# A transformer block with x transposed by the host, squares summed in place, part of w_in split by accumulating DMA, and three reordered blocks

## The chip, the cores and the metric

The kernel runs on one core of a Trainium2 chip, a few times, and each run gives the device's microseconds from start to end; the number compared is the median. One more execution is taken by the hardware profiler, and all profile lines below come from that one. Engines are named as in the profile: PE (matmul), PEld (its weight load), DVE (VectorE), ACT (ScalarE), POOL (GpSimd) and SP (SyncE, which issues most DMAs here).

## What is computed

One layer of a hybrid encoder on x of 256 x 2048, all in float32. `QK_COLS`, `ATT_WIDTH` and `CONV_CH` are 1024 columns each, so `w_in` is 2048 x 5120.

```python
xn = rms_norm(h, norm1_g[l])
proj = jnp.einsum('bsd,dn->bsn', xn, w_in[l])
q, k, v, ga, gg = jnp.split(proj, ...)
...
att = diff_attention(q, k, v, lam)          # q, k normed and rotated
u = causal_depthwise_conv(ga * sigmoid(gg), conv_w[l], conv_b[l])
u = silu(layer_norm(u, conv_ln_g[l], conv_ln_b[l]))
h = h + jnp.einsum('bsm,md->bsd', concat([att, u]), w_out[l])
hn = rms_norm(h, norm2_g[l])
a, bu = hn @ w_gate[l], hn @ w_up[l]        # 5632 hidden columns
h = h + (silu(a) * bu) @ w_down[l]
```

## The kernel before

**Precision.** [...] A product is hi x hi + lo x hi + hi x lo: three matmuls where one would do. The high part of a weight is a cast on ACT (`round_chunk`, L322), the low part a subtraction on DVE (`split_chunk`, L331). For chunks marked `by_dma` DVE is spared: ACT writes the negated high part into `wlo` (L325), and a DMA that adds, issued by POOL (L326), puts the raw weights on top.

**Chunks.** Weights are streamed in chunks of 512 KB: two blocks of 128 rows by 512 columns. Chunk 0 to 31 are the conv columns of `w_in` (four blocks of eight chunks, gate and value columns side by side, hence two loads each), 32 to 79 k, q and v, 80 to 111 `w_out`, 112 to 127 the first gate and up block. A chunk is 12 matmuls of 512 columns: eight with the high part (L361, L362), then four with the low part (L367). `run_chunks` records, for each step t, the loads, casts and subtractions of chunks ahead (two ahead, one in the first eight) and then the multiplication of chunk t; each engine runs its own list in that order. `resume` is called twice in a chunk and lets generators go on; that is how transposes, the attention and the convolution's steps are slipped between chunks.

**Buffers.** A raw chunk lies in one of five `raw` buffers; from chunk 8 on every third one lies in pool `early` (tag `wb`, two buffers) instead. There are three `whi` and three `wlo`. A load waits on SP until the last reader of its buffer is done, and all loads behind it wait too.

**The opening.** x is loaded in its rows, in five parts; PE transposes it block by block (`x_part`, L441, 32 transposes), and ACT and DVE split it, scaled by the norm's gain (`split_scaled`, L235, L236). The gains are a row table that PE transposes (L157), as are the conv weights (L184). 14 and then 5 transposes of nothing keep PE busy before the first data (L145). ACT sums squares from the rows (L430).

**The convolution** is 30 taps for each of eight channel tiles on DVE (L512, tile `y`). They are dealt out by a credit: 1.30 us a half chunk, of which a subtraction on DVE takes its part (`spend`).

**The feed-forward part** uses fast products: a *pair* chunk (kind s, `multiply_pair`) loads rows of two weight matrices (tile `wb`), forms four sums of them on DVE (`wt`, L963 to L965), casts them on ACT (`wh`) and subtracts on DVE (`wlb` L972, `wlt` L973): seven products of three matmuls (L990 to L992). Plain chunks of the two matrices are kinds g and u (`multiply_two`, L1011, L1012, L1017). `ORDER`, `FIRST_ORDER` (block 1) and `DORDERS` (down passes behind each group of gate/up blocks) say in which order the kinds come. After blocks 0 to 3, 4 to 7 and 8 to 10 stands a down pass; its results are added to the residual in DRAM by accumulating DMAs from POOL (L1135, L1152). `BY_DMA` names the g and u chunks that are split by DMA.

Of the kernel before, what the change touches and what calls it, by code (L numbers as in the profile page):

```python
# [12 lines left out]
F32 = mybir.dt.float32  # L13
# [5 lines left out]
P = 128  # L19
# [30 lines left out]

WARM = (14, 5)

XPARTS = (range(0, 2), range(2, 4), range(4, 8), range(8, 12), range(12, 16))

OPENING = KD // NK
# [24 lines left out]
ORDER = "sggsggsuusuu"  # L80
FIRST_ORDER = "gsgsggsuusuu"


HD = N // P
ND = 2
DORDERS = {4: ("gguuggsguugsuu", "sgggugggusuuuu"), 3: ("gguusggsuu", "ggsggsuuuu")}

# [23 lines left out]
def tile_block(  # L111
    ctx: ExitStack,
    tc: tile.TileContext,
    x, w_in, conv_w, w_out, w_gate, w_up, w_down, gains, vecs, rope, out,
):
# [30 lines left out]

    warm_up(WARM[0])

    rows = pre.tile([NR, P], F32, tag="rows", name="rows", bufs=1)
    act.dma_start(out=rows, in_=gains)  # L150

    act.copy(small.tile([P, 8], F32, tag="rsq", name="first"), neghalf)
    cols = const.tile([P, NR], F32, tag="cols", name="cols")

    def gain_columns():
        ps = aux_ps.tile([P, N], F32, tag="aux", name="ps_cols")
        pe.transpose(ps[:, :NR], rows, ident[:NR, :NR])  # L157
        act.copy(cols, ps[:, :NR])
# [6 lines left out]
    neg_lam = const.tile([P, 1], F32, tag="neg_lam", name="neg_lam")  # L165
    cw_rows = [pre.tile([W, N], F32, tag="va", name="cw_rows") for _ in range(CC // N)]
    rt = pre.tile([P, NM, 2, DH], F32, tag="vb", name="rt")
# [3 lines left out]
    def late_loads():  # L171
        flat = conv_w.rearrange("o w i c -> (o w i) c")
        for i in range(CC // N):
            sp.dma_start(out=cw_rows[i], in_=flat[:, i * N : (i + 1) * N])
        for t, v in ((gb, vecs[:2]), (lamv, vecs[2:])):
            sp.dma_start(out=t, in_=v.rearrange("(o v) d -> o v d", o=1).to_broadcast(list(t.shape)))
        sp.dma_start(out=rt, in_=rope.rearrange("(m p) c d -> p m c d", p=P))

    def late_constants():
        late_loads()  # L180
        yield from lag(4)
        pw = aux_ps.tile([P, N], F32, tag="aux", name="ps_cw")
        for ct in range(NCT):
            pe.transpose(pw[:, ct * W : (ct + 1) * W], cw_rows[ct * P // N][:, ct * P % N : ct * P % N + P], ident[:W, :W])  # L184
        act.copy(cw.rearrange("p c w -> p (c w)"), pw[:, : NCT * W])
        while not normed:
# [132 lines left out]

    def round_chunk(c):  # L320
        c["hi"] = c["view"](wp.tile([P, NK * N], F32R, tag="whi", name="whi", bufs=HL_BUFS))
        act.copy(c["hi"], c["raw"])  # L322
        if c["by_dma"]:
            c["lo"] = c["view"](wp.tile([P, NK * N], F32R, tag="wlo", name="wlo", bufs=HL_BUFS))
            act.activation(c["lo"], c["raw"], AF.Copy, scale=-1.0)  # L325
            pool.dma_start(out=c["lo"], in_=c["raw"].bitcast(F32R), accum_op=ALU.add)  # L326

    def split_chunk(c):
# [60 lines left out]
    def run_chunks():  # L389
# [35 lines left out]
    rstd1 = [const.tile([P, 1], F32, tag=f"rstd1_{m}", name=f"rstd1_{m}") for m in range(NM)]  # L425
    ss1 = [small.tile([P, D // N], F32, tag=f"ss1_{m}", name=f"ss1_{m}", bufs=1) for m in range(NM)]

    def square_sum(src, accum, **kw):
        junk = pre.tile([P, N], F32, tag="junk", name="junk", bufs=1)
        act.activation(junk[:, : src.shape[-1]], src, AF.Square, accum_out=accum, **kw)  # L430

    def x_load(ks):
        cs = slice(ks[0] * P, (ks[-1] + 1) * P)
        for m in range(NM):
            sp.dma_start(out=h[m][:, cs], in_=x[m * P : (m + 1) * P, cs])

    def x_part(ks):
        for k in ks:
            ps = aux_ps.tile([P, N], F32, tag="aux", name="ps_x")
            for m in range(NM):  # L440
                pe.transpose(ps[:, m * P : (m + 1) * P], h[m][:, k * P : (k + 1) * P], ident)  # L441
            xT[k] = lhs_pair("x", k)
            split_scaled(xT[k], ps[:, :S], col("g1", k))

    def x_rest():
        c = 0
        for part in XPARTS[1:]:
            while chunks_done[0] < (part[0] // NK) * 2 - 1:
                yield
            x_part(part)  # L450
            yield
            yield
            if part[-1] % (N // P) == N // P - 1:
# [608 lines left out]
    def gate_up_block(j):  # L1062
# [170 lines left out]
```

## Time and profile before

| | |
|---|---|
| median of 3 runs | 1063.49 us (1062.6 to 1063.9) |
| profiled execution, its own time | 1060.47 us |
| its span, first to last instruction | 1058.7 us |
| granted TensorE clock over the span | 0.998 |
| HBM read, written | 202.14 MB, 9.44 MB |

A timeline row is: start in us, duration, engine, line, operation, tile written <- tiles read, shapes, count; in brackets the engine's idle time just before and what ended it. A row of waits is: us in total, how often, the longest. A row of windows gives for each engine the busy time and the number of instructions, then the granted clock, the mean busy share of the DMA engines and GB/s. Durations of matmuls overlap, so the pace of PE is read from starts. Packets of DMA under 2 KB were 25806 of 123470.

### The profile page before, as it was taken

How to read it: one execution, taken by the hardware profiler on the slowest of the kernel's cores; microseconds unless marked ns; L12 is line 12 of the kernel's file. 1: busy time of each engine (PE TensorE's matmuls, PEld its weight loads, DVE VectorE, ACT ScalarE, POOL GpSimd, SP SyncE). 2: the span in 40 equal slices, each digit the busy share in tenths (PEclk: the TensorE clock that was granted, in tenths of full speed). 3: DMA queues.
4: the chain of work that ended last, by engine and by line, in shares of the span. 5: the costliest groups of instructions: out<-in, count | busy, mean ns of one | idle time of the engine just before them, and what ended most of it. 6: DMA issues, size and time to landing. Idle time of an engine off the chain costs nothing.

```text
span 1058.7 us, 13117 instructions
## 1 busy us (share of the span) xinstructions
PE 1042.8 (99%) x4702; PEld 857.3 (81%) x4702; DVE 892.2 (84%) x1087; ACT 626.3 (59%) x802; POOL 104.5 (10%) x147
## 2 busy tenths in 40 slices
PE   9999999999999999999999989999999999999998
PEld 7888888877888777888888878888888878888876
DVE  5799989899666699899687888989878788889896
ACT  6644567755766565676453656666654456667442
POOL 0030122211100100000001100000000110010010
PEclk9999999999999999999999999999999999999999
DMA  9755555553546566987857698879856889798692
GB/s 300 232 179 194 199 171 171 176 170 133 176 171 226 183 228 205 292 254 223 250 186 226 202 293 246 266 207 277 259 172 226 237 209 295 211 296 251 173 280 95
DMA packets 123470, 231.33 MB, mean 219 GB/s; under 512 B 7956, under 2 KB 25806, under 8 KB 123404
## 3 DMA queue, kind: packets, MB, share of 16 engines
q1 hardware_dynamic: 113904, 201.61, 56.3%
q0 software_dynamic: 9440, 28.84, 14.0%
q8 instruction: 37, 0.61, 0.2%
q14 instruction: 29, 0.24, 0.1%
q10 hardware_dynamic: 60, 0.03, 0.0%
HBM read 202.14 MB, written 9.44 MB: 200 GB/s over the span
## 4 chain that ended last, share of the span: by engine, by line
PE 83%; DVE 7%; DMA 3%; issue 3%; ACT 2%; POOL 2%; DVEq 0%; POOLq 0%; ACTq 0%
PE q L1017 11%; PE q L1011 11%; PE q L1012 11%; PE acc L367 9%; PE acc L362 9%; PE acc L361 9%; PE q L992 7%; PE q L990 7%; PE q L991 7%; DVE wlo L331 2%; DMA wlo<-raw 2%; DVE y L512 1%; PE ps_a L828 1%; ACT whi L322 1%; PE ps_o L724 1%
## 5 line engine op out<-in xcount | busy, mean ns | idle before, releaser
L322 ACT CAST whi<-raw 128x1024 fp32r<-128x1024 f32 x272 | 282.6, 1051 | 162.9 <-PE acc L362 56.7
L331 DVE TENSOR_TENSOR wlo<-raw,whi 128x1024 fp32r<-128x1024 f32 x234 | 283.7, 1225 | 87.5 <-ACT whi L322 85.6
L969 ACT CAST wh<-wt 128x2048 fp32r<-128x2048 f32 x52 | 99.6, 1915 | 63.4 <-DVE wt L965 62.9
L973 DVE TENSOR_TENSOR wlt<-wt,wh 128x2048 fp32r<-128x2048 f32 x52 | 119.1, 2290 | 15.0 <-ACT wh L969 14.7
L361 PE MATMUL acc<-whi,xhi 128*128 128x512 f32 x320 | 126.3, 395 | 0.5 <-ACT whi L322 0.5
L1011 PE MATMUL q<-whi,chi 128*128 128x512 f32 x320 | 125.7, 393 | 0.0
L362 PE MATMUL acc<-whi,xlo 128*128 128x512 f32 x320 | 125.0, 391 | 0.2 <-DVE xlo L236 0.2
L1012 PE MATMUL q<-whi,clo 128*128 128x512 f32 x320 | 124.8, 390 | 0.0
L990 PE MATMUL q<-wh,fhi 128*128 128x512 f32 x280 | 109.9, 393 | 0.0
L991 PE MATMUL q<-wh,flo 128*128 128x512 f32 x280 | 109.0, 389 | 0.0
L512 DVE SCALAR_TENSOR_TENSOR y<-upad,cw,y 128x256 f32<-128x256 f32 x240 | 102.8, 490 | 0.0
L1011 PE MATMUL q<-whi,ahi 128*128 128x512 f32 x256 | 100.2, 391 | 0.0
L1012 PE MATMUL q<-whi,alo 128*128 128x512 f32 x256 | 99.7, 389 | 0.0
L972 DVE TENSOR_TENSOR wlb<-wb,wh 128x1536 fp32r<-128x1536 f32 x52 | 91.1, 1753 | 5.3 <-ACT wh L966 5.3
L1017 PE MATMUL q<-wlo,chi 128*128 128x512 f32 x320 | 86.8, 393 | 5.7 <-DMA wlo<-raw 5.7
L367 PE MATMUL acc<-wlo,xhi 128*128 128x512 f32 x320 | 87.7, 396 | 0.9 <-DVE wlo L331 0.8
L966 ACT CAST wh<-wb 128x1536 fp32r<-128x1536 f32 x52 | 76.7, 1474 | 0.0
L1017 PEld LDWEIGHTS q<-wlo,chi 128*128 128x128 f32 x320 | 60.3, 189 | 19.3 <-DMA wlo<-raw 6.9
L326 POOL DMA_DIRECT2D wlo<-raw x38 | 32.8, 864 | 402.0 <-ACT wlo L325 209.5
L361 PEld LDWEIGHTS acc<-whi,xhi 128*128 128x128 f32 x320 | 60.1, 188 | 13.5 <-ACT whi L322 0.8
L362 PEld LDWEIGHTS acc<-whi,xlo 128*128 128x128 f32 x320 | 60.1, 188 | 13.2 <-DVE xlo L236 1.0
L1011 PEld LDWEIGHTS q<-whi,chi 128*128 128x128 f32 x320 | 60.4, 189 | 12.5
(229 smaller groups left out, 1782.4 us busy)
## 6 DMA issues: line engine op xcount, KB each, us to landing
raw<-in_w_down_dram SPq DMA_DIRECT2D x64, 512.0 KB, 7.4
raw<-in_w_in_dram SPq DMA_DIRECT2D x48, 512.0 KB, 4.6
raw<-in_w_gate_dram SPq DMA_DIRECT2D x48, 512.0 KB, 7.2
raw<-in_w_up_dram SPq DMA_DIRECT2D x48, 512.0 KB, 6.4
wb<-in_w_up_dram SPq DMA_DIRECT2D x40, 512.0 KB, 3.8
wb<-in_w_gate_dram SPq DMA_DIRECT2D x40, 512.0 KB, 5.0
wlo<-raw POOLq DMA_DIRECT2D x38, 512.0 KB, 6.8
raw<-in_w_in_dram SPq DMA_DIRECT2D x64, 256.0 KB, 5.6
```

Of the source, the lines that this page charges most:

```text
L322: act.copy(c["hi"], c["raw"])
L331: dve.tensor_tensor(c["lo"], c["raw"], c["hi"].bitcast(F32), ALU.subtract)
L361: pe.matmul(ps[m], xhi[:, ms], hi[:, j, :], start=c["first"] and j == 0, stop=False)
L362: pe.matmul(ps[m], xlo[:, ms], hi[:, j, :], start=False, stop=False)
L367: pe.matmul(ps[m], xhi[:, ms], lo[:, j, :], start=False, stop=c["last"] and j == nk - 1)
L512: dve.scalar_tensor_tensor(y[:, ct, :], src, wk, y[:, ct, :], ALU.mult, ALU.add)
L973: dve.tensor_tensor(lot, c["t"], c["hi"][:, :SUMMED].bitcast(F32), ALU.subtract)
L990: pe.matmul(ps, hi, c["hi"][:, w], start=bool(first), stop=False)
L991: pe.matmul(ps, lo, c["hi"][:, w], start=False, stop=False)
L1011: pe.matmul(ps, xs[i][0][:, ms], hi[:, i, :], start=i == 0 and bool(c["first"].get(qs[m])), stop=False)
L1012: pe.matmul(ps, xs[i][1][:, ms], hi[:, i, :], start=False, stop=False)
L1017: pe.matmul(sum_bank(c, qs[m]), xs[i][0][:, ms], lo[:, i, :], start=False, stop=i == 1 and bool(c["last"].get(qs[m])))
```

## The change

The host hands in x a second time, transposed and laid out by partition (`xt`), and the gains and conv weights as columns, so that no transpose of these is left. x's own rows, which the residual needs, are loaded ahead of chunks 20, 22, 24 and 26. Chunk 0 is loaded in halves, one of each from SP and ACT, and its first half is cast on DVE. The squares are taken in place of the transposed x once it is split, added up by DVE over blocks, and four matmuls with a column of ones give the sums, after chunk 10. Ten w_in chunks (16, 22 to 70) are *far*: loaded seven chunks ahead, cast and negated by ACT five chunks ahead into a `wb` buffer (tile `far`), with the low part by an accumulating DMA from POOL. No chunk before 76 uses `wb` for raw weights any more. The order of kinds in block 1 and in the second half of the last down pass has one g more ahead of a pair, and blocks 4 and 8, right behind a down pass, have no g chunk split by DMA.

```diff
-WARM = (14, 5)
+WARM = 18
+SUMS_AT = 20
+XROWS = (20, 22, 24, 26)
...
-FIRST_ORDER = "gsgsggsuusuu"
+FIRST_ORDER = "gsggsgsuusuu"
...
-DORDERS = {4: ("gguuggsguugsuu", "sgggugggusuuuu"), 3: ("gguusggsuu", "ggsggsuuuu")}
+DORDERS = {4: ("gguuggsguugsuu", "sgggugggusuuuu"), 3: ("gguusggsuu", "gggsgsuuuu")}
...
+FAR = (16, 76, 6)
+FAR_AHEAD = (7, 5)
...
-    warm_up(WARM[0])
-    rows = pre.tile([NR, P], F32, tag="rows", name="rows", bufs=1)
-    act.dma_start(out=rows, in_=gains)
...
+    warm_up(WARM)
     cols = const.tile([P, NR], F32, tag="cols", name="cols")
+    act.dma_start(out=cols, in_=gains)
...
     def late_loads():
-        flat = conv_w.rearrange("o w i c -> (o w i) c")
-        for i in range(CC // N):
-            sp.dma_start(out=cw_rows[i], in_=flat[:, i * N : (i + 1) * N])
+        sp.dma_start(out=cw, in_=conv_w)
...
-        pw = aux_ps.tile([P, N], F32, tag="aux", name="ps_cw")
-        for ct in range(NCT):
-            pe.transpose(pw[:, ct * W : (ct + 1) * W], cw_rows[ct * P // N][:, ct * P % N : ct * P % N + P], ident[:W, :W])
-        act.copy(cw.rearrange("p c w -> p (c w)"), pw[:, : NCT * W])
...
     def load_chunk(c):
...
+        if c is chunks[0]:
+            for k in range(NK):
+                x_load(range(k, k + 1))
+                for q, (col, n) in zip((sp, act), c["cols"]):
+                    q.dma_start(out=c["raw"][:, k, o : o + n], in_=rows[:, k, col : col + n])
+                    o = (o + n) % c["width"]
+            return
...
     def round_chunk(c):
...
+        if c is chunks[0]:
+            act.activation(small.tile([P, 8], F32, tag="rsq", name="first"), neghalf, AF.Sigmoid)
+            dve.tensor_copy(c["hi"][:, 0], c["raw"][:, 0])
+            x_part(range(NK))
+            act.copy(c["hi"][:, 1], c["raw"][:, 1])
+            return
+        if c in chunks[:OPENING]:
+            x_part(range(c["k0"], c["k0"] + NK))
...
+    def round_far(c):
+        t = early.tile([P, 2, NK * N], F32R, tag="wb", name="far")
+        c["hi"], c["lo"] = c["view"](t[:, 0]), c["view"](t[:, 1])
+        act.copy(c["hi"], c["raw"])
+        act.activation(c["lo"], c["raw"], AF.Copy, scale=-1.0)
+        pool.dma_start(out=c["lo"], in_=c["raw"].bitcast(F32R), accum_op=ALU.add)
...
+            for ahead, do in ((FAR_AHEAD[0], load_chunk), (FAR_AHEAD[1], round_far)):
+                if t + ahead < n and chunks[t + ahead].get("far"):
+                    do(chunks[t + ahead])
...
+    xraw = [early.tile([P, HK, S], F32, tag="wb", name="xraw") for _ in range(KD // HK)]
     def x_load(ks):
-        cs = slice(ks[0] * P, (ks[-1] + 1) * P)
-        for m in range(NM):
+        k = ks[0]
+        sp.dma_start(out=xraw[k // HK][:, k % HK : k % HK + len(ks), :], in_=xt[:, k : k + len(ks), :])
+    def x_rows(i):
+        XW = D // len(XROWS)
+        for m in range(NM):
+            cs = slice(i * XW, (i + 1) * XW)
             sp.dma_start(out=h[m][:, cs], in_=x[m * P : (m + 1) * P, cs])
     def x_part(ks):
         for k in ks:
-            ps = aux_ps.tile([P, N], F32, tag="aux", name="ps_x")
-            for m in range(NM):
-                pe.transpose(ps[:, m * P : (m + 1) * P], h[m][:, k * P : (k + 1) * P], ident)
             xT[k] = lhs_pair("x", k)
-            split_scaled(xT[k], ps[:, :S], col("g1", k))
+            split_scaled(xT[k], xraw[k // HK][:, k % HK, :], col("g1", k))
     def x_rest():
...
+        for k in range(0, KD, 4):
+            while chunks_done[0] < k + 2:
                 yield
+            act.activation(four(k), four(k), AF.Square)
+            yield
+            if k >= HK:
+                add(four(0), four(k - 4 if k == HK else k))
+                yield
+        add(four(0), four(HK))
...
+        add(t[:, :2], t[:, 2:4])
+        while chunks_done[0] < SUMS_AT:
+            yield
+        ps = aux_ps.tile([P, N], F32, tag="aux", name="ps_ss")
+        for m in range(NM):
+            for k in range(2):
+                pe.matmul(ps[:, m * 8 : m * 8 + 8], t[:, k, m * P : (m + 1) * P], ones, start=k == 0, stop=k == 1)
...
-                   BY_DMA if j > 1 else dict(g=(), u=BY_DMA["u"]))
+                   BY_DMA if j > 1 and j not in FIRSTS else dict(g=(), u=BY_DMA["u"]))
...
+    for i in range(*FAR):
+        chunks[i].update(far=True, load=lambda c: None, round=lambda c: None, split=lambda c: None)
+    last_far = FAR[1] - OPENING
     for i, c in enumerate(chunks[OPENING:-12]):
-        c["spare_raw"] = i % 3 == 2
+        c["spare_raw"] = i % 3 == 2 and i >= last_far
...
+    for i, t in enumerate(XROWS):
+        before[t] = lambda i=i: x_rows(i)
...
+    given["xt"] = given["xt"].T.reshape(KD, P, S).transpose(1, 0, 2)
+    given["conv_w"] = given["conv_w"].reshape(W, NCT, P).transpose(2, 1, 0)
```

PE's list in the opening, before, from within chunk 0 to the first matmul of chunk 1 (`xhi`, `xlo`: the parts of x; `h`: x's rows; `ps_x`: their transposes):

```order
L361 MATMUL acc<-whi,xhi_149 128x512
L362 MATMUL acc<-whi,xlo_150 128x512
L441 MATMUL ps_x<-ident,h_81 128x128
L441 MATMUL ps_x<-ident,h_82 128x128
L441 MATMUL ps_x<-ident,h_81 128x128
L441 MATMUL ps_x<-ident,h_82 128x128
L367 MATMUL acc<-wlo,xhi_149 128x512 x4
L361 MATMUL acc<-whi,xhi_193 128x512
```

And the same place in the change:

```order
L378 MATMUL acc<-whi,xhi_153 128x512
L379 MATMUL acc<-whi,xlo_154 128x512
L384 MATMUL acc<-wlo,xhi_153 128x512 x4
L378 MATMUL acc<-whi,xhi_167 128x512
L379 MATMUL acc<-whi,xlo_168 128x512
```

The four transposes between the high and the low half of chunk 0 are gone; eight more go from each of three later chunks.

DVE's list at the start of block 4, right behind the first down pass, before: the end of the first pair's low parts, the last sums of the down pass (L1151), and the second pair:

```order
L973 TENSOR_TENSOR wlt<-wt,wh 128x2048
L1151 TENSOR_TENSOR sum_5407<-q_5209,sum_5407 128x512
L1151 TENSOR_TENSOR sum_5409<-q_5274,sum_5409 128x512
L963 TENSOR_TENSOR wt<-wb 128x1024
L964 TENSOR_TENSOR wt<-wb,wt 128x512
L965 TENSOR_TENSOR wt<-wt,wb 128x512
L972 TENSOR_TENSOR wlb<-wb,wh 128x1536
L973 TENSOR_TENSOR wlt<-wt,wh 128x2048
```

And in the change:

```order
L1011 TENSOR_TENSOR wlt<-wt,wh 128x2048
L348 TENSOR_TENSOR wlo<-raw,whi 128x1024
L1189 TENSOR_TENSOR sum_5344<-q_5146,sum_5344 128x512
L1189 TENSOR_TENSOR sum_5346<-q_5211,sum_5346 128x512
L348 TENSOR_TENSOR wlo<-raw,whi 128x1024
L1001 TENSOR_TENSOR wt<-wb 128x1024
L1002 TENSOR_TENSOR wt<-wb,wt 128x512
L1003 TENSOR_TENSOR wt<-wt,wb 128x512
L1010 TENSOR_TENSOR wlb<-wb,wh 128x1536
L1011 TENSOR_TENSOR wlt<-wt,wh 128x2048
```

The two g chunks' subtractions stand ahead of the second pair's low parts.

SP's loads around chunk 28, a far one, in the change, with the semaphores that each waits for (DMASW2 is that of chunk 28's accumulating DMA; DVE, of a subtraction; two rows a chunk while the chunk is two loads of 256 columns; the row of 512 columns is the far chunk 34, and behind it come chunks 29, 30 and 31):

```order
L317 DMA raw<-in_w_in_dram 128x2x256 [waits DMAHW5_49,DVE_49]
L317 DMA raw<-in_w_in_dram 128x2x256 [waits DMAHW6_49]
L317 DMA raw<-in_w_in_dram 128x2x512 [waits DMAHW7_49,DVE_49]
L317 DMA raw<-in_w_in_dram 128x2x256 [waits DMAHW0_49,DMASW2_49,Activation_49]
L317 DMA raw<-in_w_in_dram 128x2x256 [waits DMAHW1_49]
L317 DMA raw<-in_w_in_dram 128x2x256 [waits DMAHW2_49,DVE_49]
L317 DMA raw<-in_w_in_dram 128x2x256 [waits DMAHW3_49]
```

Before, loads waited for DVE's subtractions alone; now the load of chunk 29 waits for the landing of chunk 28's low part. The same holds for chunks 47 and 59 behind 46 and 58; behind the far chunks 16, 22, 34, 52 and 64 it is the load of the chunk after the next.

More of the change, by code (lines that the diff above doesn't have):

```diff
@@ L113, in tile_block @@
     tc: tile.TileContext,
-    x, w_in, conv_w, w_out, w_gate, w_up, w_down, gains, vecs, rope, out,
+    x, xt, w_in, conv_w, w_out, w_gate, w_up, w_down, gains, vecs, rope, out,
 ):
@@ L145, in warm_up @@
             pe.transpose(warm[:, :P], ident, ident)
-    warm_up(WARM[0])
-    rows = pre.tile([NR, P], F32, tag="rows", name="rows", bufs=1)
-    act.dma_start(out=rows, in_=gains)
-    act.copy(small.tile([P, 8], F32, tag="rsq", name="first"), neghalf)
+    warm_up(WARM)
     cols = const.tile([P, NR], F32, tag="cols", name="cols")
[L155 to L158, printed above, removed]
+    act.dma_start(out=cols, in_=gains)
     def col(key, k):
@@ L165, in tile_block @@
     neg_lam = const.tile([P, 1], F32, tag="neg_lam", name="neg_lam")
-    cw_rows = [pre.tile([W, N], F32, tag="va", name="cw_rows") for _ in range(CC // N)]
     rt = pre.tile([P, NM, 2, DH], F32, tag="vb", name="rt")
@@ L425, in tile_block @@
     rstd1 = [const.tile([P, 1], F32, tag=f"rstd1_{m}", name=f"rstd1_{m}") for m in range(NM)]
-    ss1 = [small.tile([P, D // N], F32, tag=f"ss1_{m}", name=f"ss1_{m}", bufs=1) for m in range(NM)]
     def square_sum(src, accum, **kw):
@@ L1204, in tile_block @@
         before[part[0] // NK] = lambda part=part: x_load(part)
-    before[0] = lambda: (x_load(XPARTS[0]), gain_columns(), x_part(XPARTS[0]), warm_up(WARM[1]), start(x_rest()))
+    before[0] = lambda: start(x_rest())
+    for i, t in enumerate(XROWS):
+        before[t] = lambda i=i: x_rows(i)
     before[OPENING] = lambda: start(late_constants())
     run_chunks()
-_FLAT = {"x": (S, D), "w_in": (D, 5120), "conv_w": (1, W, 1, CC), "w_out": (D, D), "w_gate": (D, FF),
+_FLAT = {"x": (S, D), "xt": (S, D), "w_in": (D, 5120), "conv_w": (1, W, 1, CC), "w_out": (D, D), "w_gate": (D, FF),
          "w_up": (D, FF), "w_down": (FF, D)}
@@ L1219 @@
     arrays, args = {}, []
-    given = {name: np.asarray(inputs[name]).reshape(shape) for name, shape in _FLAT.items()}
-    given["gains"] = np.concatenate([np.asarray(inputs[name]).reshape(n, P) for name, _, n in ROWS])
+    given = {name: np.asarray(inputs["x" if name == "xt" else name]).reshape(shape) for name, shape in _FLAT.items()}
+    given["xt"] = given["xt"].T.reshape(KD, P, S).transpose(1, 0, 2)
+    given["conv_w"] = given["conv_w"].reshape(W, NCT, P).transpose(2, 1, 0)
+    given["gains"] = np.concatenate([np.asarray(inputs[name]).reshape(n, P) for name, _, n in ROWS]).T
     given["vecs"] = np.concatenate([np.asarray(inputs[name]).reshape(1, DH) for name in VECS])
```

18 lines of the change are left out of this document (8 added, 10 removed).

## The prediction, made before the changed kernel was run

> **What bounds the kernel now.** I read the page first, then who TensorE waits for.
>
> ```profile
> span 1058.7 us, 13117 instructions
> PE 1042.8 (99%) x4702; PEld 857.3 (81%) x4702; DVE 892.2 (84%) x1087; ACT 626.3 (59%) x802; POOL 104.5 (10%) x147
> PE q L1017 <- DMA wlo<-raw: 5.7, 3, 3.0
> PE q L992 <- DVE wlt L973: 1.9, 2, 1.0
> PE acc L367 <- DVE wlo L331: 0.8, 1, 0.8
> ```
>
> PE is busy 99% of the span, so a microsecond counts only if it leaves PE's queue: a matmul or transpose less, or a wait less. The three waits shown are 8.4 us. Next, the timeline gives PE's pace: from a pair's first matmul to the next chunk stand 21 matmuls (7 products of 3).
>
> ```profile
> 875.71 0.39 PE L990 MATMUL q<-wh,fhi 128*128 128x512 f32 x1
> 880.47 0.39 PE L1011 MATMUL q<-whi,chi 128*128 128x512 f32 x1
> ```
>
> 4.76 us / 21 = 0.227 us each: a chunk of 12 takes 2.72 us, a pair 4.76. The change has the same number of such matmuls, so I look for places where PE kept another pace.
>
> **1. The opening.** Timeline and one window, from the warm-up to the first matmul of chunk 8:
>
> ```profile
> 0.72 0.54 ACTq L150 DMA_DIRECT2D rows<-in_gains_dram  x1
> 0.72 3.33 DMA rows<-in_gains_dram
> 1.35 3.25 PE L145 MATMUL ps_warm<-ident 128*128 128x128 f32 x14 [1.35 <-POOL neghalf L139]
> 7.43 0.50 PE L361 MATMUL acc<-whi,xhi 128*128 128x512 f32 x1 [0.51 <-ACT whi L322]
> 12.24 1.05 ACT L322 CAST whi<-raw 128x1024 fp32r<-128x1024 f32 x1 [1.60 <-DMA raw<-in_w_in_dram]
> 13.09 1.03 PE L441 MATMUL ps_x<-ident,h 128*128 128x128 f32 x8
> 13.88 1.18 PE L367 MATMUL acc<-wlo,xhi 128*128 128x512 f32 x4
> 15.08 0.49 PE L361 MATMUL acc<-whi,xhi 128*128 128x512 f32 x1
> 33.65 0.39 PE L361 MATMUL acc<-whi,xhi 128*128 128x512 f32 x1
> 7.43:33.65 26.22, 25.96 (x124) 20.85 (x125) 17.03 (x25) 19.40 (x39) 2.35 (x4) 1.00 0.94 299
> ```
>
> Chunks 0 to 7 take 26.2 us where 8 x 2.72 = 21.8 would do; 28 of the 32 transposes stand in there, eight in 13.88 - 13.09 = 0.79 us, so 2.8 us. They go. The warm-up becomes 18, which by 14 in 3.25 us ends near 5.5 us, so chunk 0 can begin about 2 us earlier; the gains (landed at 4.05 us) and ACT's two further DMA issues of half a microsecond stand beside the warm-up. But the row at 12.24 says that chunk 2's weights come by DMA, and the bytes ahead of them stay the same (x is only transposed); the window's DMA share is 0.94. So I let DMA set chunk 2: cast at 12.24 to 13.3, matmuls at 13.3 instead of 15.08. From there six chunks need 16.3 us: chunk 8 at 29.6, **4.0 us earlier**. Bounds: without any DMA wait chunk 8 comes at 5.5 + 21.8 = 27.3 (6.3 us); 2.4 us if a wait there is followed by a spell of slow clock, whose 1.6 us is worked out in part 4. The squares (four of 1024 columns instead of eight of 512) and DVE's four adds (three of 1024 columns, one of 512; a subtraction of 1024 takes 1.2 us in part 2, so 4.3 us) hide beside this: ACT is busy 19.4 and DVE 17.0 of 26.2 us. Without that cover the adds would cost those 4.3 us, but they are spread over five chunks. The x rows that the residual needs come later, by SP, and nobody reads them before the output projection.
>
> ```profile
> 38.28 0.68 PE L184 MATMUL ps_cw<-ident,cw_rows 31*128 31x31 f32 x8
> 38.89 1.20 PE L367 MATMUL acc<-wlo,xhi 128*128 128x512 f32 x4
> ```
>
> The eight conv-weight transposes, 0.6 us, go; four ps_ss matmuls come, which no row shows: 0.08 us each by these (0.3 in all), 0.1 by the transposes above. Net **0.2 us**, between 0 and 0.6.
>
> **2. Every sixth w_in chunk by DMA.** DVE loses ten subtractions of 1.2 us. They were hidden, since PE waited for a wlo only once, at 217.8, where DVE's taps stood ahead of it.
>
> ```profile
> 216.62 1.27 DVE L512 SCALAR_TENSOR_TENSOR y<-upad,cw,y 128x256 f32<-128x256 f32 x3
> 217.80 1.22 DVE L331 TENSOR_TENSOR wlo<-raw,whi 128x1024 fp32r<-128x1024 f32 x1
> 219.08 1.19 PE L367 MATMUL acc<-wlo,xhi 128*128 128x512 f32 x4 [0.84 <-DVE wlo L331]
> ```
>
> PE's step there was 1.0 us too long. Chunk 70 now leaves DVE, and taps end earlier since a far chunk spends no credit: **1.0 us**, bounds 0 and 1.2. What it adds: two ACT passes, a POOL issue and a DMA, each far ahead.
>
> ```profile
> L326 POOL DMA_DIRECT2D wlo<-raw x38: 845/862/936, 416.1 to 978.6; - x38
> DMA to landing us min/median/max: 4.7/6.8/11.7
> 51.08 1.06 ACT L322 CAST whi<-raw 128x1024 fp32r<-128x1024 f32 x1 [1.67 <-PE acc L362]
> 57.23 0.39 PE L361 MATMUL acc<-whi,xhi 128*128 128x512 f32 x1
> raw<-in_w_in_dram SPq DMA_DIRECT2D x64, 256.0 KB, 5.6
> ```
>
> A chunk's cast (16 in these rows) starts 6.15 us ahead of its matmuls; a far one stands three chunks earlier in ACT's order, 14.3 us ahead. After two ACT passes of 1.06 us and the median landing of 6.8 its low part is there 5.4 us early. But its raw buffer is held till then, and in three places (chunks 29, 47, 59) the load of the very next chunk waits for it on SP, with all later loads behind: 5.6 us plus a cast of 1.06 end 1.3 us after the far chunk's start, 1.5 us before they are needed. In five more the load is that of the chunk after, with 4.2 us to spare. So nothing, if landings stay under 8.3 us.
>
> **3. Two orders.** In both blocks a pair's first wlt was late.
>
> ```profile
> 403.86 2.29 DVE L973 TENSOR_TENSOR wlt<-wt,wh 128x2048 fp32r<-128x2048 f32 x1 [0.31 <-ACT wh L969]
> 406.21 0.50 PE L992 MATMUL q<-wlt,fhi 128*128 128x512 f32 x1 [1.03 <-DVE wlt L973]
> 1026.79 2.29 DVE L973 TENSOR_TENSOR wlt<-wt,wh 128x2048 fp32r<-128x2048 f32 x1
> 1029.13 0.50 PE L992 MATMUL q<-wlt,dhi 128*128 128x512 f32 x1 [0.88 <-DVE wlt L973]
> ```
>
> One g chunk more ahead of the pair gives PE 2.72 us and costs DVE one wlo, 1.2. The waits of 1.0 and 0.9 (steps 1.2 and 1.0 too long) go. The next pair then follows after one g only: DVE needs 1.2 + 0.7 + 0.7 + 1.75 + 2.3 + 0.3 (ACT) + 1.2 = 8.15 us per pair and g, PE 33 x 0.227 = 7.5; of the 0.65 the lead just won covers most. **1.6 us**, bounds 0.9 (nothing covered, twice) and 2.2.
>
> **4. No accumulating DMA for g in the blocks behind a down pass.** The two long waits are there.
>
> ```profile
> 612.29 0.39 PE L1012 MATMUL q<-whi,clo 128*128 128x512 f32 x1
> 615.71 1.20 PE L1017 MATMUL q<-wlo,chi 128*128 128x512 f32 x4 [3.03 <-DMA wlo<-raw]
> 867.63 0.39 PE L1012 MATMUL q<-whi,clo 128*128 128x512 f32 x1
> 870.46 2.07 PE L1017 MATMUL q<-wlo,chi 128*128 128x512 f32 x4 [2.44 <-DMA wlo<-raw]
> 873.89 0.40 PE L1011 MATMUL q<-whi,chi 128*128 128x512 f32 x1
> 605.89 0.39 PE L990 MATMUL q<-wh,fhi 128*128 128x512 f32 x1
> 606.02 1.28 DVE L1151 TENSOR_TENSOR sum<-q,sum 128x512 f32<-128x512 f32 x2
> 611.87 2.29 DVE L973 TENSOR_TENSOR wlt<-wt,wh 128x2048 fp32r<-128x2048 f32 x1 [0.31 <-ACT wh L969]
> ```
>
> The first costs 3.2 us and a second short wait behind it 0.3. The second costs 2.6, and then eight matmuls take 873.89 - 870.46 = 3.43 us instead of 1.82: 1.6 us at half pace. Together 7.7 us. What is late next: DVE gets two wlo ahead of the second pair, so its wlt ends at 614.2 + 2.4 = 616.6, and PE asks for it at 605.89 + (21 + 24 + 2) x 0.227 = 616.6. I give back 0.2 each: **7.3 us**, bounds 5.2 (a whole wlo of 1.25 us late in each block) and 7.7.
>
> [...] These rows differ: 2.44 us sufficed once, 3.03 us did not. [...]
>
> **Sum.** 4.0 + 0.2 + 1.0 + 1.6 + 7.3 = 14.1 us, from the profiled execution's 1060.5 to 1046.4. The median shown is 1063.5, 3.0 above it; I keep that distance: **1049.4 us**.
>
> **Rivals.**
> - *The opening meets the slow clock.* PE now waits for chunks 1 and 2, about a microsecond each; if that halves the pace once, as at 870, the opening gains 2.4 instead of 4.0: 1051.0. For it: the wait at 12.24. Against: at 615 nothing followed. Chance 0.17.
> - *The raw buffers become the wait.* 2 MB of x rows are loaded over chunks 20 to 26 as well. If landings take 10 us there, the three next-chunk loads are 1.7 us late, and with a slow clock after each 3.3: 1059.3. Chance 0.10.
> - *Slower than before.* The same place: at 11.1 us per landing three waits of 2.8 + 1.6 us eat 13.2 us and the five two-behind places begin; at the longest landing seen, 11.7, it is 3 x 5.0 + 5 x 0.7 = 18.5 us: 1067.9. It decides at about 11.2 us; the median of 6.8 speaks against. Chance 0.05.
> - *Nothing moves net*: DVE is the next bound behind the down passes and in both orders, so that sections 3 and 4 bring half (4.5 us) and the far chunks lose the rest: 1063. Chance 0.04.
>
> **How the numbers follow.** Forecast 0.64, rivals as given. 0.2% (2.1 us) is about what can be told from no change: faster 0.91, same 0.04, slower 0.05. The range: all upper bounds (6.3 + 0.6 + 1.2 + 2.2 + 7.7 = 18.0) give 1045.5, a slow clock that also followed the wait at 615 in the timed runs 1.6 less; upwards I take in the first rival (1.6) and the lower bounds of 1's conv weights, 2, 3 and 4 (0.2 + 1.0 + 0.7 + 2.1), to 1055.0, and one microsecond of far landings a little over 8.3 us: 1043.5 to 1056.
>
> **What would show it.** Right: no wait of the low-part matmuls (L1017 before) for a DMA near 600 and 855, chunk 8's first matmul near 29.6 us, far landings under 8 us, no PE wait between 40 and 240. Wrong: PE waiting for wlt behind the down passes, SP waiting for far landings with ACT idle for raw, granted clock under 1 in the first 35 us.

## The result, and the profile after

The change makes the kernel faster: 1052.17 us median against 1063.05 of the kernel before in the same rounds, ratio 0.9899 (95% interval 0.9882 to 0.9916). A second set of rounds gave 1052.36 us, 0.9907 (0.9891 to 0.9922). 1049.4 was forecast, within 1043.5 to 1056, which holds it. The profiled execution took 1051.97 us. Its page and the waits of PE (us in total, times, longest):

```profile
span 1050.2 us, 13065 instructions
PE 1036.5 (99%) x4668; PEld 853.0 (81%) x4668; DVE 889.5 (85%) x1084; ACT 628.0 (60%) x794; POOL 107.2 (10%) x154
PE acc L384 <- DVE wlo L348: 3.4, 2, 1.9
PE acc L378 <- ACT whi L331: 2.3, 3, 1.2
PE q L1030 <- DVE wlt L1011: 0.2, 1, 0.2
```

The waits for the accumulating DMAs and nearly all of that for wlt are gone, as forecast. The two rows for wlo and whi are new in size: 5.7 us, where the kernel before had 0.8 us for wlo. So the span fell by 8.5 us, not by 14.1.

To find where, I compare the start of the same matmul in both traces. Since both run the same 512-column matmuls in the same order up to the pairs, the difference is **PE's lead** over the kernel before. Two fences with the first matmuls of chunks 60, 72 and 96 (timelines of PE, before and after):

```profile
183.80 0.39 PE L361 MATMUL acc<-whi,xhi 128*128 128x512 f32 x1
220.46 0.48 PE L361 MATMUL acc<-whi,xhi 128*128 128x512 f32 x1
300.97 0.39 PE L361 MATMUL acc<-whi,mchi 128*128 128x512 f32 x1
```
```profile
179.48 0.39 PE L378 MATMUL acc<-whi,xhi 128*128 128x512 f32 x1
220.13 0.48 PE L378 MATMUL acc<-whi,xhi 128*128 128x512 f32 x1
301.67 0.39 PE L378 MATMUL acc<-whi,mchi 128*128 128x512 f32 x1
```

The lead is 4.3 us at chunk 60, 0.3 at chunk 72 and -0.7 at chunk 96. The whole gain of the opening is given back there, and more. The table has this for all kernels of the study (us; block 1 is read behind its pairs, blocks 4 and 8 behind their second pair; spans of one profiled execution each).

| kernel | chunk 8 | 60 | 66 | 75 | 81 | 96 | block 1 | block 4 | block 8 | span |
|---|---|---|---|---|---|---|---|---|---|---|
| changed | 4.1 | 4.3 | 2.6 | 0.3 | 0.3 | -0.7 | 0.3 | 4.1 | 8.3 | 1050.2 |
| changed, again | 4.0 | 4.2 | 2.4 | 0.2 | 0.2 | -0.8 | -0.4 | 3.3 | 7.5 | 1051.2 |
| 1: no far chunks | 2.4 | 2.7 | 2.7 | 2.6 | 2.5 | -4.2 | -3.8 | 0.0 | 3.6 | 1054.9 |
| 2: far 16 to 58 | 3.7 | 3.9 | 3.9 | 3.4 | 3.4 | -0.8 | 0.5 | 4.3 | 8.4 | 1050.2 |
| 3: far 17 to 71 | 4.2 | 4.1 | 4.0 | 3.9 | 3.9 | 2.8 | 3.9 | 7.6 | 11.8 | 1046.7 |
| 4: passes, no far | 4.1 | 4.3 | 2.9 | 0.2 | 0.2 | -6.7 | -6.6 | -2.8 | 1.3 | 1057.1 |
| 5: passes later | 4.1 | 3.1 | 0.9 | -2.9 | -2.9 | -3.9 | -2.9 | 0.9 | 5.0 | 1053.5 |
| 6: no far, fewer taps | 4.3 | 4.5 | 4.5 | 4.6 | 3.7 | 2.5 | 3.5 | 7.2 | 11.4 | 1047.5 |
| 7: taps held back | 3.8 | 4.1 | 3.4 | 2.9 | 2.8 | 0.4 | 1.3 | 5.1 | 9.3 | 1049.2 |
| 8: far 18 to 72 | 4.2 | -6.5 | -6.5 | -8.2 | -8.2 | -9.3 | -8.3 | -4.5 | -0.4 | 1058.8 |
| 9: orders and DMAs as before | 4.1 | 4.4 | 2.6 | -1.3 | -1.3 | -2.3 | -2.6 | -3.1 | -3.4 | 1062.3 |

(Experiment 1 starts 1.7 us lower through a spell of slow clock in its opening, granted clock 0.50 from 11.09 to 14.10 us.) Now the place of the loss, around chunk 61, in the trace after: first PE's three waits of the stage, then ACT, POOL and DVE (start, duration, what, and in brackets the idle time before and who ended it).

```profile
191.61 0.73 PE L384 MATMUL acc<-wlo,xhi 128*128 128x512 f32 x2 [1.49 <-DVE wlo L348]
208.78 0.50 PE L378 MATMUL acc<-whi,xhi 128*128 128x512 f32 x1 [1.17 <-ACT whi L331]
218.74 1.19 PE L384 MATMUL acc<-wlo,xhi 128*128 128x512 f32 x4 [1.93 <-DVE wlo L348]
```
```profile
168.52 4.04 DVE L550 SCALAR_TENSOR_TENSOR y<-upad,cw,y 128x256 f32<-128x256 f32 x10
172.48 2.36 DVE L348 TENSOR_TENSOR wlo<-raw,whi 128x1024 fp32r<-128x1024 f32 x2
180.41 1.23 DVE L348 TENSOR_TENSOR wlo<-raw,whi 128x1024 fp32r<-128x1024 f32 x1 [4.02 <-ACT whi L331]
...
171.00 3.89 POOL L211 TENSOR_SCALAR rsq<-ssq 128x4 f32<-128x4 f32 x1 [1.95 <-ACT junk L449]
176.46 0.19 POOL L211 TENSOR_SCALAR rsq<-ssq 128x4 f32<-128x4 f32 x1
...
176.42 1.14 ACT L654 ACTIVATE qn<-acc,fq 128x128 f32<-128x128 f32 x4 [2.73 <-POOL fq L650]
177.43 1.06 ACT L341 CAST far<-raw 128x1024 fp32r<-128x1024 f32 x1
178.36 1.09 ACT L342 ACTIVATE far<-raw 128x1024 fp32r<-128x1024 f32 x1
179.32 1.06 ACT L331 CAST whi<-raw 128x1024 fp32r<-128x1024 f32 x1
```

Read it upwards from PE: it waits 1.49 us for a wlo. DVE had been busy without pause since 180.41, and before that idle for 4.02 us, waiting for ACT's cast of chunk 61. That cast starts at 179.32, because ahead of it stand the two passes for far chunk 64 (1.9 us), and ahead of these the scaling `qn` of k, which waited 2.73 us for POOL. POOL's small scale took 3.89 us instead of the 0.19 of its next run, and ended when DVE's unbroken row of ten taps and two subtractions did (172.48 + 2.36 = 174.84; POOL at 171.00 + 3.89 = 174.89).

What holds POOL until then is not shown by these rows: they show that its operation ends 0.05 us after DVE's row. Experiment 7 shortens that row.

### The profile page after: what moved, and what is told of

Read it like the earlier page. It is cut to its first block, busy times and chain, and to the rows that moved or that the text cites. A ratio compares the mean times of both kernels' runs of the same rounds, so it can differ in the third digit from the quotient of the medians.

```text
span 1050.2 us, 13065 instructions
## 1 busy us (share of the span) xinstructions
PE 1036.5 (99%) x4668; PEld 853.0 (81%) x4668; DVE 889.5 (85%) x1084; ACT 628.0 (60%) x794; POOL 107.2 (10%) x154
## 4 chain that ended last, share of the span: by engine, by line
PE 62%; DVE 2%; DMA 1%; ACT 0%; issue 0%; DVEq 0%
PE q L1055 12%; PE q L1049 12%; PE q L1050 12%; PE q L1030 8%; PE q L1028 8%; PE q L1029 8%; PE ps_a L866 1%; DMA raw<-in_w_down_dram 1%; PE acc L384 1%; PE acc L379 1%; PE acc L378 1%; DVE wlo L348 1%; DVE wlt L1011 0%; DVE wt L1001 0%; ACT wh L1007 0%
## 5 line engine op out<-in xcount | busy, mean ns | idle before, releaser
L331 ACT CAST whi<-raw 128x1024 fp32r<-128x1024 f32 x261 | 270.0, 1050 | 138.7 <-PE q L1050 48.0
L348 DVE TENSOR_TENSOR wlo<-raw,whi 128x1024 fp32r<-128x1024 f32 x228 | 275.9, 1223 | 85.0 <-ACT whi L331 84.3
L378 PE MATMUL acc<-whi,xhi 128*128 128x512 f32 x280 | 111.4, 398 | 2.3 <-ACT whi L331 2.3
L379 PE MATMUL acc<-whi,xlo 128*128 128x512 f32 x280 | 109.5, 391 | 0.0
L384 PE MATMUL acc<-wlo,xhi 128*128 128x512 f32 x280 | 76.7, 396 | 3.4 <-DVE wlo L348 3.4
L1050 PEld LDWEIGHTS q<-whi,clo 128*128 128x128 f32 x320 | 60.1, 188 | 12.3
L1055 PE MATMUL q<-wlo,ahi 128*128 128x512 f32 x256 | 68.7, 389 | 0.0
L335 POOL DMA_DIRECT2D wlo<-raw x34 | 29.4, 866 | 380.1 <-ACT wlo L334 218.7
```

What stands on the lines that cost most here:

```text
L348: dve.tensor_tensor(c["lo"], c["raw"], c["hi"].bitcast(F32), ALU.subtract)
L378: pe.matmul(ps[m], xhi[:, ms], hi[:, j, :], start=c["first"] and j == 0, stop=False)
L379: pe.matmul(ps[m], xlo[:, ms], hi[:, j, :], start=False, stop=False)
L1050: pe.matmul(ps, xs[i][1][:, ms], hi[:, i, :], start=False, stop=False)
L1055: pe.matmul(sum_bank(c, qs[m]), xs[i][0][:, ms], lo[:, i, :], start=False, stop=i == 1 and bool(c["last"].get(qs[m])))
```

## The experiments

**Theory A**: the two ACT passes of a far chunk stand in ACT's queue ahead of casts for which DVE and PE then wait. **Rival B**: DVE, busy 44 to 47 of every 50 us there, is the bound, and the opening's lead can't last whatever ACT does. Four kernels against each other.

**1. No far chunks.**

```diff
-FAR = (16, 76, 6)
+FAR = (28, 28, 6)
```

> The changed kernel without the far chunks (all their low parts by DVE again, spare raw buffers from chunk 28 on); the opening, the orders and the blocks behind a down pass as changed. Theory A: PE's lead of 4.3 us over the kernel before was lost between chunks 60 and 85 because a far chunk's two ACT passes (2 us) stand in ACT's queue ahead of a cast that DVE or PE then waits for. By A the waits of 1.5, 1.2 and 1.9 us at 190, 207 and 217 us fall to the one of about 1 us that the kernel before had, and the span is 1045 to 1046.5 us instead of 1050.2. Rival B: DVE, busy 44 to 47 of every 50 us there, bounds the stage whatever the opening wins; then ten subtractions more (12 us) on DVE leave the span at 1050 or above, to 1056, with longer waits for wlo.

1055.86 us, ratio 0.9937 (0.9922 to 0.9952), span 1054.9. Both theories are half right. Between chunks 60 and 81 the lead stays (2.7 to 2.5), as A says. But then 6.7 us go between 81 and 96, which A did not expect. PE's waits there, and the taps of the three kernels (duration, then first and last start in us; before, after, without far chunks):

```profile
PE ps_ln L608 <- ACT upad L599: 2.8, 2, 2.4
PE acc L378 <- DVE mchi L615: 1.6, 1, 1.6
```
```profile
L512 DVE SCALAR_TENSOR_TENSOR y<-upad,cw,y x240: 469/484/695, 43.8 to 270.4; 128x256 f32<-128x256 f32 x120
```
```profile
L550 DVE SCALAR_TENSOR_TENSOR y<-upad,cw,y x240: 468/482/680, 45.6 to 253.0; 128x256 f32<-128x256 f32 x120
```
```profile
L550 DVE SCALAR_TENSOR_TENSOR y<-upad,cw,y x240: 460/478/682, 47.3 to 277.1; 128x256 f32<-128x256 f32 x120
```

The last tap starts at 277 us instead of 253; the layer norm behind them (`ps_ln`) and its result (`mchi`), an operand of the output projection, come late. So B's bound is there, but at the end of the taps. The new opening starts them later: the first tap starts at 45.6 instead of 43.8 us though PE is 4.5 us ahead, 6.3 us later by PE's count, since by the code it needs the sums of squares, which now come after chunk 10. That this late start is what makes the end late is argued; no run here moved the sums. Of the 6.7 us some 1.5 are a spell of slow clock behind the waits shown (seven steps of PE take 3.1 us from 291.2 us on, in place of 1.6; granted clock 0.54 from 291.7 to 294.5 us).

**2. Eight far chunks, 64 and 70 through DVE.**

```diff
-FAR = (16, 76, 6)
+FAR = (16, 64, 6)
```

> The changed kernel with eight far chunks (16 to 58): 64 and 70 go through DVE. A: only those two stood where they hurt, since the lead is still 4.3 us at chunk 60; span 1045 to 1047 us. B: DVE has 2.4 us more to do in its tightest place: span 1050 to 1053 us.

1054.43 us, 0.9925 (0.9907 to 0.9944), span 1050.2. The loss between 60 and 72 is nearly gone (3.9 to 3.4), as A says, and a loss of 4.2 us between 81 and 96 takes its place: its last tap starts 2 us later than the changed kernel's (255.3 us), while PE is 3 us further on. (The profiled execution is the fastest of its four; the median lies 2.4 us above it.)

**3. Far chunks 17 to 71.**

```diff
-FAR = (16, 76, 6)
+FAR = (17, 77, 6)
```

> The changed kernel with ten far chunks, each one chunk later (17 to 71), so that each pair of ACT passes stands 2.7 us later. A: what counts is the place; the first of the two hurtful pairs falls into the 3.4 us in which ACT was idle from 185 us on, so that at least its wait of 1.5 us goes: span 1046.5 to 1049 us. B: DVE's work is the same: span 1050 us within 0.7.

1049.14 us, 0.9880 (0.9865 to 0.9894), span 1046.7: 0.2 us lost between chunks 60 and 75 and 1.0 between 81 and 96.

**4. The passes alone.** No far chunks, and two ACT passes into a spare tile where chunks 64 and 70 had theirs.

```diff
+            if t + FAR_AHEAD[1] in (64, 70):
+                for scale in (1.0, -1.0):
+                    act.activation(scratch, ..., AF.Copy, scale=scale)
```

> The kernel without far chunks, and two ACT passes over 1024 columns into a tile that nobody reads at each of the two places where chunks 64 and 70 had theirs. A: the passes alone bring the loss back: span 3 to 5 us above that of the kernel without far chunks, 1048 to 1051 us. B: ACT has room (busy 33 of 50 us), so the same as without them within 0.7 us.

1058.97 us, 0.9971 (0.9961 to 0.9980), span 1057.1. The medians lie 3.1 us above those of experiment 1, the spans 2.2 (3 to 5 were expected), with 1.7 us of slow clock (granted 0.50) in experiment 1's opening. The lead between two chunks is free of that: 4.3 at chunk 60, 0.2 at chunk 75. The passes alone cost 4.1 us there, as much as in the changed kernel (4.0). That part of A is shown.

**The changed kernel and far chunks 17 to 71, in the same rounds.**

> The changed kernel unaltered, as the measure for the others of this call: span about 1050.2 us, with a loss of 4 us of PE's lead over the kernel before between chunks 60 and 72 and of 1.0 us between chunks 81 and 96.

> Far chunks 17 to 71 once more, beside the changed kernel in the same rounds. If it is the place of the ACT passes that counts, 2.5 to 3.5 us below the changed kernel in the medians; if the single look was luck of the opening, within 1 us of it.

1052.36 and 1049.58 us, spans 1051.2 and 1046.7. 17 to 71 is 2.8 us faster; its ratio to the kernel before is 0.9880 (0.9864 to 0.9897) against 0.9907 (0.9891 to 0.9922). It is the fastest full version of the study.

**5. The same far chunks, passes one chunk later.**

```diff
-FAR_AHEAD = (7, 5)
+FAR_AHEAD = (7, 4)
```

> The same far chunks as in the changed kernel (16 to 70), loaded as early, but with their two ACT passes and their DMA one chunk later in the order (four chunks ahead instead of five). Theory A (the passes stand ahead of a cast that DVE waits for): the loss between chunks 60 and 72 falls from 4.0 to under 1 us, span 1046.5 to 1048 us; the low parts still land 3.5 us early at the median landing. Rival (which chunks are far matters, for DVE's order of subtractions and taps, not when ACT passes over them): 1050.2 us within 0.7.

1053.14 us, 0.9916 (0.9902 to 0.9931), span 1053.5: a miss, 6.0 us lost between chunks 60 and 75. The passes now stand behind the cast of chunk 61, at the same step as in experiment 3, and it is no better. So the place of the passes alone does not decide it. (Some 1.5 us of the loss is slow clock behind a wait of 1.93 us: 0.50 from 222.3 to 224.9 us.) Nor did the passes move alone: their DMA moved with them. The low part of far chunk 58 landed at 167.84 us (162.34 in the changed kernel), SP's load behind it was issued at 167.89, and ACT stood for it, so that the cast of chunk 59 started at 171.57 us instead of 168.06, and everything behind it on ACT and POOL was later too. How much of the loss is due to that was not separated:

```profile
171.57 1.05 ACT L331 CAST whi<-raw 128x1024 fp32r<-128x1024 f32 x1 [2.23 <-DMA raw<-in_w_in_dram]
```

The traces also differ in what comes ahead: in experiment 3 far chunk 59 takes its subtraction out of DVE's row just ahead of POOL's scales. There POOL's scale took 1.53 us and `qn` did not wait; here 2.71 us (3.89 in the changed kernel), and `qn` waited 1.55 us.

```profile
171.30 1.53 POOL L211 TENSOR_SCALAR rsq<-ssq 128x4 f32<-128x4 f32 x1 [0.80 <-ACT junk L449]
```
```profile
174.53 2.71 POOL L211 TENSOR_SCALAR rsq<-ssq 128x4 f32<-128x4 f32 x1 [3.13 <-ACT junk L449]
178.76 1.14 ACT L654 ACTIVATE qn<-acc,fq 128x128 f32<-128x128 f32 x4 [1.55 <-POOL fq L650]
```

**6. Is it DVE's work that makes the late loss?** No far chunks and 32 of the 240 taps left out.

```diff
-            side.append(deque((lambda k=k, ct=ct: tap(k, ct)) for k in range(1, W)))
+            side.append(deque((lambda k=k, ct=ct: tap(k, ct)) for k in (*range(1, W - 5), W - 1)))
```

> Without far chunks, and with 32 of the convolution's 240 taps left out (four of 30 for each of the eight column groups), which takes 32 x 0.4 = 12.8 us from DVE, about what the ten far subtractions did. Theory B, as it now stands: without far chunks DVE's last tap ends late (277.6 us instead of 253.5), the layer norm behind it is late, and PE loses 6.7 us between chunks 84 and 96. By B PE's lead at chunk 96 is then 1 to 2 us below that at chunk 84 instead of 6.7, and the span 1047 to 1050 us. If something else of the far chunks mattered there (buffers, loads), the loss of 6.7 us stays and the span is about 1055.

1049.23 us, span 1047.5. The last tap starts at 246 us, and between chunks 81 and 96 PE loses 1.2 us instead of 6.7. The buffers and loads are as in experiment 1, so it is DVE's work, B's part.

**7. Taps held back.** If DVE's unbroken row holds POOL, and POOL holds ACT, a shorter row must help without moving any pass.

```diff
+    for i in (58, 64, 70):
+        chunks[i]["split"] = lambda c: spend(LO_US * 2)
```

> The changed kernel, but for chunks 58, 64 and 70 the convolution's taps are held back as much as if DVE had subtracted there (7 taps instead of 10 in the run at 168.5 us). Theory A2: DVE's unbroken run of taps and two subtractions kept POOL's small scale (3.89 us instead of 0.19) and with it ACT's row of work and two far passes back; with a run 1.2 us shorter ACT's wait for POOL falls from 2.7 to about 1.5 us and the loss between chunks 60 and 72 from 4.0 to 1.5 to 3 us: span 1047.5 to 1049.2 us. Rival: the four microseconds are just the ACT passes, whatever POOL does: 1050.2 us within 0.7.

1051.15 us, 0.9899 (0.9884 to 0.9913), span 1049.2. POOL's scale and ACT's wait for it shrink as expected, and the loss between 60 and 72 falls from 4.0 to 1.2 us. The first of PE's three waits falls from 1.49 to 0.33 us, and up to there DVE's rows differ by those three taps alone. Behind it the taps held back at chunks 64 and 70 also shorten DVE's own row, which this run doesn't separate:

```profile
171.25 2.71 POOL L211 TENSOR_SCALAR rsq<-ssq 128x4 f32<-128x4 f32 x1 [1.94 <-ACT junk L449]
175.49 1.14 ACT L654 ACTIVATE qn<-acc,fq 128x128 f32<-128x128 f32 x4 [1.56 <-POOL fq L650]
178.40 1.06 ACT L331 CAST whi<-raw 128x1024 fp32r<-128x1024 f32 x1
```

The last tap starts at 258 instead of 253 us for it, and 2.4 us go between chunks 81 and 96: the two losses trade against each other. In the medians the gain over the changed kernel, 1.0 us, is too small to be told.

The cast of chunk 61 gathers all this (in the kernel before it starts at 181.20 us, and `qn` waited 1.21 us for POOL):

```profile
180.18 1.14 ACT L616 ACTIVATE qn<-acc,fq 128x128 f32<-128x128 f32 x4 [1.21 <-POOL fq L612]
181.20 1.06 ACT L322 CAST whi<-raw 128x1024 fp32r<-128x1024 f32 x1
```

Its start, counted from PE's start of chunk 60, and the loss from chunk 60 to 66:

| kernel | passes | cast of 61 from PE's chunk 60 | loss 60 to 66 |
|---|---|---|---|
| 3: far 17 to 71 | behind it | 175.95 - 179.75 = -3.8 | 0.0 |
| before | none | 181.20 - 183.80 = -2.6 | 0.0 |
| 1: no far chunks | none | 178.71 - 181.14 = -2.4 | 0.0 |
| 2: far 16 to 58 | none | 177.86 - 179.88 = -2.0 | 0.0 |
| 7: taps held back | ahead | 178.40 - 179.72 = -1.3 | 0.6 |
| 5: passes later | behind it | 179.78 - 180.67 = -0.9 | 2.2 |
| 4: passes, no far | ahead | 179.05 - 179.49 = -0.4 | 1.5 |
| changed | ahead | 179.32 - 179.48 = -0.2 | 1.8 |

In these eight traces, two microseconds or more ahead cost nothing. Where it is later PE pays, and where the passes follow it (5) they delay the next cast on top.

**8. Far chunks 18 to 72.**

> Ten far chunks once more, 18 to 72. If it is by chance of place that 17 to 71 lost 0.3 us and 16 to 70 lost 4.0 us between chunks 60 and 72, this one lies anywhere between 0 and 5 us, span 1046 to 1052 us; if only the distance of the passes behind the chunk before counts, it is no worse than 17 to 71, 1046.7 us.

1061.61 us, 0.9991 (0.9982 to 1.0001), span 1058.8: outside both expectations, and by another mechanism. 7.3 us go at once at chunks 24 to 27, in a wait of PE and slow pace behind it (rows of SP's waits, of ACT and of PE; the matmul at 83.63 us takes 0.63 us, as those at a granted clock of 0.50 in experiment 1 do, where those before the wait take 0.39):

```profile
SPq L317 <- DMA far<-raw: 50.0, 10, 14.0
```
```profile
81.94 1.04 ACT L331 CAST whi<-raw 128x1024 fp32r<-128x1024 f32 x1 [14.40 <-DMA raw<-in_w_in_dram]
```
```profile
83.04 0.79 PE L378 MATMUL acc<-whi,xhi 128*128 128x512 f32 x1 [4.79 <-ACT whi L331]
83.63 0.63 PE L379 MATMUL acc<-whi,xlo 128*128 128x512 f32 x1
```

SP stood 14.0 us behind the landing of one far chunk's low part, and every later load with it. In the changed kernel the longest such wait is 6.6 us; ACT waits behind it (4.76 us, for the raw weights of a cast at 82.85 us), PE does not.

The trace shows why one step decides between the two (rows of ACT, POOL and SP in this run):

```profile
62.06 1.05 ACT L342 ACTIVATE far<-raw 128x1024 fp32r<-128x1024 f32 x1
71.03 0.88 POOL L343 DMA_DIRECT2D far<-raw  x1
75.67 1.92 SPq L317 DMA_DIRECT2D raw<-in_w_in_dram  x4
```

ACT's passes were done at 63.1 us, but POOL issued the DMA only at 71.03: ahead of it in POOL's queue stood the tables for the rotation of q and k (L188 to L194, from 61.30 us on). In the changed kernel POOL issues a far chunk's DMA at 55.65 us, before these tables, and the next one at 72.39, 3.56 us after they were done. It is a queue again that decides, here POOL's.

**9. Orders and accumulating DMAs as before**, with the new opening and the far chunks.

```diff
-                   BY_DMA if j > 1 and j not in FIRSTS else dict(g=(), u=BY_DMA["u"]))
+                   BY_DMA if j > 1 else dict(g=(), u=BY_DMA["u"]))
-FIRST_ORDER = "gsggsgsuusuu"
+FIRST_ORDER = "gsgsggsuusuu"
...
```

> The changed kernel with the three orders and the accumulating DMAs behind a down pass as before; opening and far chunks as changed. If the trace is read rightly, PE's waits of 3.8 us near 607 and 4.2 us near 866 come back, and those of 1.05 and 0.5 us at the pairs of block 1 and of the last down pass: span 1050.2 + 9.5 = 1059 to 1060.5 us. If those gains hung on something else (on where the blocks start, say), less than 7 us come back.

1063.33 us, 1.0015 (1.0006 to 1.0025), span 1062.3. The waits are back (PE, us, times, longest):

```profile
PE q L1055 <- DMA wlo<-raw: 5.0, 2, 2.6
PE q L1030 <- DVE wlt L1011: 1.9, 2, 1.1
```

From chunk 96 to the end the lead falls by 1.1 us, where the changed kernel gains 9.4; so 10.5 us hang on these parts, 1.0 more than expected, since both waits for the DMA are followed by slow clock here (0.50 from 618.6 to 621.6 and from 874.7 to 877.7 us). Another 1.6 us went at chunk 72, where the wait of 1.9 us was followed by it too (0.55 from 218.7 to 222.3 us). What remains says most: opening and far chunks by themselves leave the kernel where it was (PE is 2.3 us behind at chunk 96, of which 1.6 are that spell).

## Why the prediction was right or wrong, point by point

- **The opening, 4.0 us: right**, step by step. DMA set chunk 2, its cast at 12.02 (forecast 12.24), matmuls at 13.12 (13.3), chunk 8 at 29.57 (29.6):

```profile
12.02 1.05 ACT L331 CAST whi<-raw 128x1024 fp32r<-128x1024 f32 x1 [0.60 <-DMA raw<-in_w_in_dram]
13.12 0.50 PE L378 MATMUL acc<-whi,xhi 128*128 128x512 f32 x1 [0.69 <-ACT whi L331]
29.57 0.39 PE L378 MATMUL acc<-whi,xhi 128*128 128x512 f32 x1
35.01 0.95 PE L493 MATMUL ps_ss<-ones,xraw 128*128 128x8 f32 x8
```

  The lead grows by 0.4 us more up to chunk 15 (forecast 0.2), though the sums take eight matmuls in 0.8 us, not four in 0.3. What failed is a sentence beside it, that the adds and squares hide. They hide in the opening, but the taps behind them start 6.3 us later by PE's count. Without far chunks the end of the taps then costs 6.7 us, 240 us later (experiment 6 shows that it is DVE's work that sets it; that the late start is passed on to the end is argued).
- **The far chunks, 1.0 us: wrong, and this is the step that failed.** The lead went from 4.5 to -0.7: 5.2 us lost in place of 1.0 won. Of the ten subtractions I said that they were hidden, and of the two ACT passes that they stand "far ahead". I followed the far chunk's own deadline and its buffer, and both held (landings of 6.0 us median and 7.9 at most, under the 8.3 of the forecast). I did not follow what stands behind the passes on ACT: a near cast that stood 2.6 us ahead of PE's chunk 60 in the kernel before, where the loss begins somewhere between 2.0 and 1.3: about one microsecond to spare. The two passes take 1.9 of it, and `qn`, which waits for POOL, starts 0.6 later by PE's count (176.42 - 179.48 = -3.06, before 180.18 - 183.80 = -3.62). Experiment 4 shows the passes' 4 us; experiment 7 shows POOL's part in the first of the three waits. The remaining 1.0 us between chunks 81 and 96 is also in experiment 3; its cause was not isolated. The far chunk's own two conditions after the change (landing of its DMA; SP's waits for it, us, times, longest):

```profile
DMA to landing us min/median/max: 5.1/6.0/7.9
SPq L317 <- DMA far<-raw: 35.9, 10, 6.6
```

- **Two orders, 1.6 us: right**, 1.1 + 0.5. The last pair's wait did not go wholly: the next one, one g behind, waits, as the working had it.

```profile
1030.63 0.50 PE L1030 MATMUL q<-wlt,dhi 128*128 128x512 f32 x1 [0.22 <-DVE wlt L1011]
```

- **Blocks 4 and 8, 7.3 us: mechanism right, a little more**, 3.8 + 4.2 = 8.0, above the bound of 7.7. The wlt of the second pair came just in time, at 616.1 (forecast 616.6), so the 0.2 us that I gave back twice was not lost:

```profile
613.83 2.29 DVE L1011 TENSOR_TENSOR wlt<-wt,wh 128x2048 fp32r<-128x2048 f32 x1 [0.32 <-ACT wh L1007]
616.28 0.40 PE L1030 MATMUL q<-wlt,fhi 128*128 128x512 f32 x1
```

- **The sum**: 4.1 + 0.4 - 5.2 + 1.5 + 8.0 = 8.8 us, against 8.7 at the last matmul. The median gained more, 10.9 us. I had kept a distance of 3.0 us between median and profiled execution; after the change it is 0.2. That fits slow clock behind both DMA waits in the timed runs of before, of which its profile has one and experiment 9's both. The granted clock of the timed runs points the same way: 0.997 in the median of the 39 of the kernel before in the experiments' rounds, which two spells of 3.4 us at half pace would make (an estimate from the one of 3.41 us in its profile), 0.998 in its profile, which has one and in its last 0.7 us the start of another, and 0.998 to 1.000 in the eight of the changed kernel. Where in those runs the spells fell has no trace, so the cause is not shown. So the terms missed by 5.3 us, and some 2 of these were made up by a gain that the working did not have: that the median came this near is in part luck.
- **The rivals.** Slow clock in the opening: not in the changed kernel's traces, but in experiment 1's (below), 1.7 us. Raw buffers as the wait: PE does not wait for them in the change, but does in experiment 8, one step beside it, with landings no longer than 7.3 us. Of the signs of being right, "no PE wait between 40 and 240" was the one that failed, and it named the place. Of the signs of being wrong, SP at a far landing with ACT idle for raw was there (4.76 us before 82.85 us), but it cost PE nothing.

## What to carry to other kernels

When work is moved to an engine that is "60% busy", ask what stands behind it in that engine's queue and how many microseconds the tightest of it has to spare; the moved work's own deadline is the lesser question. This holds for each engine that the moved work passes through: in experiment 8 it was POOL's queue. A lead won early is kept only if every engine that feeds a later stage is early too: name the next place where another engine's total work sets the time, here the end of the taps, before counting it. And comparing the start of the same instruction along both traces shows in one column which part of a change pays and which takes back.

## What the runs showed of the hardware

Whether a wait of PE was followed by slow clock is not a matter of its length alone. Followed by it were the 2.44 us of the kernel before (granted clock 0.50 from 870.3 to 873.7 us); experiment 9's 2.46, 2.56 and 1.9 us (0.50, 0.50 and 0.55 in the stretches given there); experiment 5's 1.93 us (0.50 from 222.3 to 224.9 us); and the 2.39 us of experiment 1, with 0.38 and 1.64 us just behind them (0.54 from 291.7 to 294.5 us). Not followed by it were the 3.03 us of the kernel before (1.00 from 615.7 to 619.0 us) and the 1.93 us of the changed kernel (1.00 from 218.7 to 225.9 us). One spell in experiment 1 followed a wait of 1.55 us in the opening (a window: length, busy time by engine, granted clock, DMA):

```profile
11.09:14.10 3.01, 3.01 (x9) 2.32 (x8) 2.11 (x4) 2.80 (x6) 0.00 (x0) 0.50 1.06 385
```

It may matter where the wait falls. In the kernel before, the spell at half clock lasts from 870.30 to 873.71 us, 3.41 us, and the next begins at 1058.03 us, after PE's last matmul: 187.73 us later, 55 steps of 3.413 us. Counted back from 870.30 in such steps, the 2.44 us of waiting lie 2.28 in one step, and the 3.03 us lie across two, 1.62 and 1.41. That is a fit to two waits of one trace, and no run tested it.

POOL was held for far longer than its own work: 3.89 us for an operation that took 0.19 us the next time, until a row of twelve DVE instructions ended; with three taps less in the row (experiment 7) it was 2.71 us. It is not held each time: in the changed kernel an operation on 128x1 took 0.30 us within the same row, from 168.75 us on (DVE's ten taps start at 168.52). What holds POOL and what lets it in was not followed up.

```profile
168.75 0.30 POOL L205 TENSOR_SCALAR neg_lam<-neg_lam 128x1 f32<-128x1 f32 x1
```
